# A bias table's load and the first part of its product moved to the head of a hybrid decoder layer

## The chip, the cores and the metric

The kernel runs on one core of a Trainium2 chip. Its metric is the device time of one execution in microseconds (us); of several runs the median counts. The engines are TensorE (PE; its weight loads are shown apart as PEld), VectorE (DVE), ScalarE (ACT), GpSimd (POOL) and SyncE (SP). SP and ACT also issue DMAs, each on a queue of its own: the trace calls SP's q1 and ACT's q10, and marks an issue with SPq or ACTq.

## The reference

One decoder layer on 1024 tokens of width 1024, with 16 meta tokens put in front. Cut to its outline:

```
h = layer_norm(concat([meta, x]), in_ln_g, in_ln_b)
z = h @ w_in + b_in                       # q | k | v | conv value, conv gate | merge gates
# attention: banded blocks of 128 queries, window 128, 16 meta keys, a sink per head
s = q @ k * scale + rel_bias[t5_bucket(q_pos - k_pos)]     # masked outside the window
o = softmax(s, sink) @ v ;  y_attn = o @ w_attn_proj
c = silu(layer_norm(dwconv31(c_val * sigmoid(c_gate)))) @ w_conv_proj
h = layer_norm(ALPHA*h + (sigmoid(g_a)*y_attn + sigmoid(g_c)*c) @ w_out)
f = (gelu(dwconv3(h @ w_up_gate)) * dwconv3(h @ w_up_u)) @ w_down
h = layer_norm(ALPHA*h + f)               # the 16 meta tokens are dropped
```

The bias `rel_bias[t5_bucket(d)]` depends on the distance alone. So the kernel makes one row of 564 values for each of the 8 heads, `vrow`, as a product of two parts of one small table `tab`: 33 rows that hold a one-hot matrix of 564 columns (bucket by distance; row 33 is the mask) and, in 8 more columns, the bias of each bucket and head.

## The kernel before

Everything is float32, and accurate products are made from two halves of each operand (hi and lo, three products for one). Tokens lie in 9 tiles: `xm` holds the meta tokens, and x0 to x7 hold 128 tokens each. The program has a head (to about 54 us), in which the tokens are normalised, turned by PE (transposes at L500) and multiplied by the first three tiles of `w_in` (L547 and L550), then a stretch with the other tiles of `w_in`, the convolution over 31 taps on DVE and the attention (to about 390 us), then the two projections, `w_out` and the feed-forward part.

A scheduler of the framework sets each engine's order of work at build time, by priorities (`rank`, `tc.cur_priority`) and a simulated timeline. In the head the order is written out by hand instead: the wrappers `pe`, `ac`, `dv` and `po` tie each instruction of an engine to the one written before it. PE begins with 23 products of a 128x128 matrix of ones with itself into the tile `ps_w` (L574). Nothing reads them; they occupy PE while the first tokens are loaded and normalised. PE's next instructions are the transposes of `turns(0, ...)`: for each of four column blocks one of `xm` and two of the normalised tiles `xn`. ACT's first instructions in the head are `table(0)`, the inverse root of the meta tokens' variance (L417), which waits for DVE's statistics, and `norm(0, ...)` (L466), which waits for POOL's small steps (`newton(0)`).

The first loads are all SP's, in the order of their ranks: meta tokens, x0, x1, `cols` (biases and the identity matrix of the transposes), a weight tile, x2, x3, x4, two weight tiles, x5, x6, x7, then the table at rank 25 as the 14th, then two `gb` (L113; 512 KB each but for the meta tokens with 64 KB, `cols` with 259 KB and the table with 73.7 KB). Each DMA takes one of eight semaphores in turn (DMAHW0 to DMAHW7 in the rows below), and the DMA that takes the same one again waits for the earlier to land. So SP's 14th DMA, the table, waits for the sixth, x2; the first `gb` for x3, the second `gb` for x4.

The two products of the table stand behind the last product of the head:

```
for a, b in ((0, 400), (400, J_LEN)):                       # J_LEN = 564
    ps = pat.tile([P, 512], F, name="ps_v", tag="o" if a == 0 else "t", bufs=1 if a == 0 else 2)
    after(nc.tensor.matmul(ps[:NH, :b - a], tab[:, J_LEN:], tab[:, a:b], start=True, stop=True), pe_done[-1])
    after(nc.vector.tensor_copy(vrow[:, a:b], ps[:NH, :b - a]), first_nm)
load(v1d, vrow)
```

`vrow` goes to DRAM (`v1d`), from there to 128 copies (`vd`), and from these the skewed bias tiles are loaded, which the attention adds to its scores. All of `tab` but the 33 loaded rows is set to zero by POOL (L204), so the product runs over 128 partitions.

Of the kernel before, what the change touches and what calls it, by code (L numbers as in the profile page):

```python
# [23 lines left out]
F = mybir.dt.float32  # L24
# [5 lines left out]
P = 128  # L30
# [8 lines left out]
NH = 8  # L39
# [29 lines left out]
J_BAND, J_META, J_META0, J_METAQ, J_LEN = 0, 384, 400, 544, 564  # L69
# [32 lines left out]
def tile_hybrid_layer(  # L102
# [3 lines left out]
    nc = tc.nc  # L106
# [5 lines left out]
    def load(o, i):  # L112
        return nc.sync.dma_start(out=o, in_=i)  # L113

    def store(o, i):

        return nc.scalar.dma_start(out=o, in_=i)
# [4 lines left out]
    def after(ins, first):  # L122

        tc.add_manual_dep(ins.ins, first.ins.name, mybir.DependencyInfo(
            mybir.DependencyClass.NoSync, mybir.DependencyReason.SCHED_ONLY), reason="order of work")

    @contextmanager
    def rank(p):

        saved = tc.cur_priority  # L130
        tc.cur_priority = p
        yield
        tc.cur_priority = saved
# [30 lines left out]
    pat = ps_stack.enter_context(tc.tile_pool(name="pat", bufs=1, space=PSUM, reuse_waits="tile"))  # L164
# [3 lines left out]
    start = ExitStack()  # L168
# [33 lines left out]
    tab = sp.tile([P, J_LEN + NH], F, name="tab")  # L202
    with rank(0):
        nc.gpsimd.memset(tab, 0.0)  # L204
    with rank(25):
        load(tab[:33], table_in)

    def bcol(m):
        return colA[:, m:m + 1]
# [189 lines left out]
    def src_of(j):  # L399
        return (xt[j], P) if j >= 0 else (xm[:2 * NMETA], 2 * NMETA)  # L400
# [13 lines left out]
    def table(t):  # L414
        mv, t_, r_, m_ = norms[t]
        n = src_of(tokens[t][0])[1]
        ac(nc.scalar.activation(r_[:n], mv[:n, :, 1], AF.Abs_reciprocal_sqrt, bias=eps[:n], scale=1.0))  # L417

    def half_var(t):
        n = src_of(tokens[t][0])[1]  # L420
        mv, t_ = norms[t][:2]
        put, ts = (po, nc.gpsimd.tensor_scalar) if t < 2 else (dv, V.tensor_scalar)
        put(ts(t_[:n], mv[:n, :, 1], EPS, -0.5, OP.add, OP.mult))

    def newton(t):
        n = src_of(tokens[t][0])[1]
        mv, t_, r_, m_ = (x_[:n] for x_ in norms[t])
        if t < 3:
            put, ts = (po, nc.gpsimd.tensor_scalar) if t < 2 else (dv, V.tensor_scalar)
            put(ts(t_, t_, r_, r_, OP.mult, OP.mult))  # L430
            put(ts(t_, t_, 1.5, r_, OP.add, OP.mult))
            if t < 2:
                put(ts(m_, mv[:, :, 0], -1.0, t_, OP.mult, OP.mult))
            return
        stt = V.scalar_tensor_tensor
        dv(stt(t_, mv[:, :, 1], EPS, r_, OP.add, OP.mult))
        dv(stt(t_, t_, -0.5, r_, OP.mult, OP.mult))
        dv(stt(r_, t_, 1.5, r_, OP.add, OP.mult))
        dv(stt(m_, mv[:, :, 0], -1.0, r_, OP.mult, OP.mult))
# [7 lines left out]
    def norm(t, j, on_dve, cols=range(0, D, 512)):  # L447
        x_, n = src_of(j)
        i = tokens[t].index(j)
        mv, t_, r_, m_ = norms[t]  # L450
        if j < 0:
            xns[j], to = xm, xm[96:]
        elif cols[0]:
            to = xns[j]
        else:
            xns[j] = to = sp.tile([P, D], F, name="xn", tag="xn", bufs=4) if j < 4 else OB[:, (j - 4) * D:(j - 3) * D]
        if t < 3:
            r_ = t_
        for a in cols:
            if on_dve:  # L460
                s1, s2, o1, o2 = r_[:n, i:i + 1], m_[:n, i:i + 1], OP.mult, OP.add
                if t == 2:
                    s1, s2, o1, o2 = mv[:n, i, 0:1], s1, OP.subtract, OP.mult
                dv(V.tensor_scalar(to[:, a:a + 512], x_[:, a:a + 512], s1, s2, o1, o2))
            else:
                ac(nc.scalar.activation(to[:, a:a + 512], x_[:, a:a + 512], AF.Identity, bias=m_[:n, i:i + 1],  # L466
                                        scale=r_[:n, i:i + 1]))
# [102 lines left out]

    tc.cur_priority = RK_START
    warm = pat.tile([P, 512], F, name="ps_w", tag="o")
    for i in range(23):
        pe(nc.tensor.matmul(warm[:, :P], ones, ones, start=True, stop=True))  # L574
    stat(0, -1)
    half_var(0)
    table(0)
    newton(0)
    norm(0, -1, False, (0,))
    stat(1, 0)  # L580
# [64 lines left out]

    tc.cur_priority = RK_RESID + 1000
    vrow = sp.tile([NH, J_LEN], F, name="vrow")
    for a, b in ((0, 400), (400, J_LEN)):
        ps = pat.tile([P, 512], F, name="ps_v", tag="o" if a == 0 else "t", bufs=1 if a == 0 else 2)
        after(nc.tensor.matmul(ps[:NH, :b - a], tab[:, J_LEN:], tab[:, a:b], start=True, stop=True), pe_done[-1])  # L650
        after(nc.vector.tensor_copy(vrow[:, a:b], ps[:NH, :b - a]), first_nm)
    load(v1d, vrow)

# [79 lines left out]
    for r in range(2):  # L733
        rows = slice(r * HD, (r + 1) * HD)

        def put(o, j, skew=1):
            load(o[rows], dram(vd, r * J_LEN + j, [[L8 - skew, HD], [2 * J_LEN, NH // 2], [1, o.shape[-1]]]))
# [8 lines left out]
    ps = pat.tile([P, 512], F, name="ps_vm", tag="t", bufs=2)  # L746
# [4 lines left out]
    for q4 in range(2):  # L751
        ps = pat.tile([P, 512], F, name="ps_v4", tag="t", bufs=2)
# [41 lines left out]
    ps = pat.tile([P, 512], F, name="ps_s2", tag="t", bufs=2)  # L794
    for h in range(NH):
        g, r = divmod(h, 4)
        o = ps[:2, h * 16:(h + 1) * 16]
# [34 lines left out]
    for g in range(NKV):  # L832
        ps = pat.tile([P, 512], F, name="ps_t2", tag="t", bufs=2)
# [6 lines left out]
    for g in range(NKV):  # L840
        o = po[:, g * 8:g * 8 + 8]
# [21 lines left out]
    for i in range(NB):  # L863
        for g in range(NKV):
# [7 lines left out]
            for u in range(2):  # L872
                k0 = 144 * (i - 1) + 16 + HD * u if i else 0
                w = KW - first[u]
                ps = pat.tile([P, 512], F, name="ps_s", tag="s", bufs=2)
                for h in range(2):
                    o = ps[:, h * KW:h * KW + w]
                    for j in range(2):
                        nc.tensor.matmul(o, q[:, j, u, h], kflat[:, k0:k0 + w],
                                         start=j == 0, stop=j == 1)  # L880
# [27 lines left out]
            for n, cols_of in ((P, (0, 80)), (80, (P, 0))):  # L908
                ps = pat.tile([P, 512], F, name="ps_t", tag="t", bufs=2)
# [659 lines left out]
    for c in range(FC):  # L1569
# [8 lines left out]
        for subs in passes:  # L1578
            last = subs == passes[-1]
            w_next = iter(range(7))  # L1580
            a, b = SUB[subs[0]][0], SUB[subs[-1]][1]
            i = max(a, 2)
# [348 lines left out]
```

## Time and profile before

| | |
|---|---|
| median of 3 runs | 1236.25 us (1236.25 to 1236.26) |
| the profiled execution's own time | 1236.54 us |
| its span, first to last instruction | 1234.6 us |
| PE busy | 1225.2 us, 99% of the span |
| DVE busy | 1085.2 us, 88% |
| ACT busy | 584.7 us, 47% |
| mean HBM traffic | 172 GB/s |

The page gives shares of the span for each engine, the span in 40 slices, the DMA queues, the chain of work that ended last and the costliest groups of instructions. Other views are asked of the trace: the waits by engine, the timeline of a short window (start, length, engine, line, tile, and in brackets the idle time before and what ended it), the busy time by windows, and the packets of each DMA queue in a window. Two records of a float32 product stand for one instruction (the 23 idle products are 46 records).

### The profile page before, as it was taken

Reading aid. Unit: us, or ns where it says so; the run is one execution under the profiler, and the core shown is the slowest. Engines: PE = TensorE matmul, PEld = TensorE weight load, DVE = VectorE, ACT = ScalarE, POOL = GpSimd, SP = SyncE. Lnnn points to the kernel's source line nnn. Section 1 sums busy time; section 2 is a strip of 40 time slices with the busy share of each in tenths; the row PEclk is TensorE's granted clock in tenths of the full one; section 3 lists DMA queues with packets and bytes.
Section 4 is the critical chain, followed back from the end, with each engine's and each line's share of the span. In section 5 each row is a group of like instructions: output and inputs, shape, how many; then the busy total and the mean of one; then the engine's idle time right before and its main releaser. Section 6 shows DMA issues by size and latency. Waiting matters only on the chain.

```text
span 1234.6 us, 21810 instructions
## 1 busy us (share of the span) xinstructions
PE 1225.2 (99%) x8568; PEld 1141.5 (92%) x8568; DVE 1085.2 (88%) x1842; ACT 584.7 (47%) x1065; POOL 15.6 (1%) x20
## 2 busy tenths in 40 slices
PE   9999999999999999999999999999999999999997
PEld 8999989999999999888999999999999998888886
DVE  8899989999879798659899999998999986996697
ACT  7532336654255223345755545555455554445331
POOL 1000000000000010000000000000000000000000
PEclk9999999999999999999999999999999999999999
DMA  7396834412255655322255555554455568988722
GB/s 282 74 298 151 210 98 116 127 55 73 82 158 163 183 140 144 104 85 87 66 171 207 191 187 205 188 183 142 172 203 190 178 239 304 391 315 312 256 86 85
DMA packets 109152, 213.02 MB, mean 173 GB/s; under 512 B 31883, under 2 KB 46779, under 8 KB 108922
## 3 DMA queue, kind: packets, MB, share of 16 engines
q1 hardware_dynamic: 93050, 200.56, 49.5%
q10 hardware_dynamic: 16000, 11.07, 2.9%
q8 instruction: 67, 1.10, 0.4%
q14 instruction: 35, 0.29, 0.1%
HBM read 149.98 MB, written 62.70 MB: 172 GB/s over the span
## 4 chain that ended last, share of the span: by engine, by line
PE 98%; DVE 1%; ACT 0%; issue 0%; DMA 0%; POOL 0%; DVEq 0%; POOLq 0%
PE px L1599 14%; PE py L1599 9%; PE ps_x L1745 9%; PE ps_z L315 8%; PE ps_z L314 8%; PE ps_z L310 8%; PE ps_z L1745 8%; PE pw L1599 5%; PE pz L1599 5%; PE ps_p L310 2%; PE ps_p L314 2%; PE ps_p L315 2%; PE ps_w L310 2%; PE ps_w L315 2%; PE ps_w L314 2%; PE ps_z L550 2%
## 5 line engine op out<-in xcount | busy, mean ns | idle before, releaser
L707 DVE SCALAR_TENSOR_TENSOR FA<-cin,cols,FA 128x1026 f32<-128x1026 f32 x120 | 152.2, 1277 | 0.9
L315 PE MATMUL ps_z<-RHO,wlo 128*128 128x256 f32 (+2 forms) x324 | 103.5, 320 | 0.0
L314 PE MATMUL ps_z<-RHO,whi 128*128 128x256 f32 (+2 forms) x324 | 103.4, 319 | 0.0
L315 PE MATMUL ps_z<-RHC,wlo 128*128 128x256 f32 (+2 forms) x324 | 103.4, 319 | 0.0
L314 PE MATMUL ps_z<-RHC,whi 128*128 128x256 f32 (+2 forms) x324 | 103.4, 319 | 0.0
L310 PE MATMUL ps_z<-RHO,whi 128*128 128x256 f32 (+2 forms) x324 | 103.3, 319 | 0.0
L310 PE MATMUL ps_z<-RHC,whi 128*128 128x256 f32 (+2 forms) x324 | 103.2, 319 | 0.0
L279 ACT CAST whi<-wr 128x1024 fp32r<-128x1024 f32 x37 | 38.9, 1050 | 107.4 <-PE ps_z L314 85.5
L1408 ACT CAST RHO<-wr 128x512 fp32r<-128x512 f32 x92 | 55.3, 619 | 25.3 <-DVE wr L1426 11.7
L1409 DVE TENSOR_TENSOR RHO<-wr,RHO 128x512 fp32r<-128x512 f32 x92 | 61.8, 684 | 5.1 <-ACT RHO L1408 5.0
L310 PEld LDWEIGHTS ps_z<-RHO,whi 128*128 128x128 f32 x324 | 60.9, 188 | 4.3
L314 PEld LDWEIGHTS ps_z<-RHO,whi 128*128 128x128 f32 x324 | 61.0, 188 | 4.2
L310 PEld LDWEIGHTS ps_z<-RHC,whi 128*128 128x128 f32 x324 | 60.9, 188 | 4.1
L314 PEld LDWEIGHTS ps_z<-RHC,whi 128*128 128x128 f32 x324 | 61.0, 188 | 4.0
L315 PEld LDWEIGHTS ps_z<-RHO,wlo 128*128 128x128 f32 x324 | 60.9, 188 | 4.0
L315 PEld LDWEIGHTS ps_z<-RHC,wlo 128*128 128x128 f32 x324 | 61.0, 188 | 3.9
L1426 DVE TENSOR_TENSOR wr<-wr 128x512 f32<-128x512 f32 x88 | 59.9, 681 | 0.2
L282 DVE TENSOR_TENSOR wlo<-wr,whi 128x1024 fp32r<-128x1024 f32 x35 | 42.7, 1220 | 11.8 <-ACT whi L279 11.4
L1611 ACT COPY FA<-px 128x514 f32<-128x514 f32 (+2 forms) x23 | 13.2, 572 | 70.7 <-PE px L1599 70.6
L1408 ACT CAST ws<-wr 128x512 fp32r<-128x512 f32 x60 | 36.1, 618 | 18.8 <-DVE wr L1426 10.7
L714 ACT ACTIVATE FA<-ps_z,cols 128x258 f32<-128x258 f32 (+2 forms) x48 | 26.1, 544 | 39.4 <-PE ps_z L315 36.6
L1599 PE MATMUL px<-OA,RHO 128*128 128x258 f32 (+1 forms) x336 | 43.8, 279 | 0.0
(491 smaller groups left out, 3488.2 us busy)
## 6 DMA issues: line engine op xcount, KB each, us to landing
wr<-in_w_up_dram SPq DMA_DIRECT2D x44, 512.0 KB, 4.6
wr<-in_w_z_dram SPq DMA_DIRECT2D x30, 512.0 KB, 3.9
fd<-FA SPq DMA_DIRECT2D x44, 256.0 KB, 2.4
OB<-in_w_down_dram SPq DMA_DIRECT2D x19, 512.0 KB
qt<-qd SPq DMA_DIRECT2D x28, 256.0 KB, 4.1
td<-OB SPq DMA_DIRECT2D x12, 512.0 KB
sums<-fd SPq DMA_DIRECT2D x12, 512.0 KB, 7.6
sd<-sums SPq DMA_DIRECT2D x12, 512.0 KB
```

What stands on the lines that cost most here:

```text
L279: ins = nc.scalar.copy(hi, raw)
L282: return (nc.vector if quick else nc.gpsimd).tensor_tensor(lo, raw, f32(hi), OP.subtract)
L310: ins = nc.tensor.matmul(ps, ah, bh, start=i == 0, stop=False)
L314: nc.tensor.matmul(ps, ah, bl, start=False, stop=False)
L315: last = nc.tensor.matmul(ps, al, bh, start=False, stop=i == n - 1)
L707: nc.vector.scalar_tensor_tensor(acc[c], cin[:, j:j + U], wc, acc[c], OP.mult, OP.add)
L714: nc.scalar.activation(t, ps, AF.Tanh, bias=bcol(14 + i), scale=0.5)
L1408: nc.scalar.copy(hi, src)
L1409: ins = nc.vector.tensor_tensor(lo, src, f32(hi), OP.subtract)
L1426: ins = nc.vector.tensor_tensor(*x)
L1599: ins = nc.tensor.matmul(o, x[:, ks], bmat(sub, q, hl, k), start=first and k + j == 0, stop=k == 3 and j == 2, skip_group_check=not first)
L1745: nc.tensor.matmul(bank[:, cs], l[:, ts], r[:, ws], start=first and a and x + k == 0, stop=z and x == len(ops) - 1 and k == 2, skip_group_ ...
```

## The change

The table's load leaves SP's list and becomes a DMA of ACT, written behind `table(0)`. The idle products become 20. Behind them PE makes the first 512 columns of the table's product, into the bank that `ps_w` had. The other 52 columns stay where both products were. DVE copies the 512 columns as soon as its own head is done, and the 52 columns as before.

```
-    with rank(25):
-        load(tab[:33], table_in)
...
-    for i in range(23):
+    for i in range(20):
         pe(nc.tensor.matmul(warm[:, :P], ones, ones, start=True, stop=True))
     stat(0, -1)
     half_var(0)
     table(0)
+    ac(store(tab[:33], table_in))
+    ps_v0 = pat.tile([P, 512], F, name="ps_v", tag="o")
+    pe(nc.tensor.matmul(ps_v0[:NH], tab[:, J_LEN:], tab[:, :512], start=True, stop=True))
     newton(0)
...
-    for a, b in ((0, 400), (400, J_LEN)):
-        ps = pat.tile([P, 512], F, name="ps_v", tag="o" if a == 0 else "t", bufs=1 if a == 0 else 2)
-        after(nc.tensor.matmul(ps[:NH, :b - a], tab[:, J_LEN:], tab[:, a:b], start=True, stop=True), pe_done[-1])
+    for a, b in ((0, 512), (512, J_LEN)):
+        ps = ps_v0
+        if a:
+            ps = pat.tile([P, 512], F, name="ps_v", tag="t", bufs=2)
+            after(nc.tensor.matmul(ps[:NH, :b - a], tab[:, J_LEN:], tab[:, a:b], start=True, stop=True), pe_done[-1])
         after(nc.vector.tensor_copy(vrow[:, a:b], ps[:NH, :b - a]), first_nm)
```

(`store` issues a DMA from ACT, `load` from SP.) In the changed kernel line numbers between L207 and L574 are two lower, and from L651 on three higher.

PE at the start of the program, before (with what each instruction waits for; the DMAHW names are the DMAs' semaphores):

```order
L574 MATMUL ps_w<-ones_r 128x128 [waits DVE_49]
L574 MATMUL ps_w<-ones_r 128x128 x22
L500 MATMUL ps_h_216<-cols,xm 128x128 [waits DMAHW0_49,DMAHW3_49,DVE_49,Activation_49]
L500 MATMUL ps_h_216<-cols,xn 128x128 [waits Activation_49]
L500 MATMUL ps_h_216<-cols,xn 128x128 [waits DVE_49]
```

PE at the same place, now:

```order
L572 MATMUL ps_w<-ones_r 128x128 [waits DVE_49]
L572 MATMUL ps_w<-ones_r 128x128 x19
L578 MATMUL ps_v<-tab 8x512 [waits DMAHW7_49,PE_49,Pool_49]
L498 MATMUL ps_h_215<-cols,xm 128x128 [waits DMAHW0_49,DMAHW3_49,DVE_49,Activation_49]
L498 MATMUL ps_h_215<-cols,xn 128x128 [waits Activation_49]
```

The table's product stands ahead of all transposes and waits for the table's DMA (DMAHW7).

ACT at the start of the program, before (`sq` is a first call that loads ACT's function table, `r_...` an inverse root, `xm` the meta tokens):

```order
L174 ACTIVATE sq<-eps 128x1 [waits DVE_49]
L417 ACTIVATE r_172<-mv_170,eps 32x1 [waits DVE_49]
L466 ACTIVATE xm<-xm,m_173,t_171 32x512 [waits DMAHW0_49,Pool_49]
L417 ACTIVATE r_186<-mv_184,eps 128x1 [waits DVE_49]
L466 ACTIVATE xm<-xm,m_173,t_171 32x512
```

ACT at the same place, now:

```order
L174 ACTIVATE sq<-eps 128x1 [waits DVE_49]
L415 ACTIVATE r_168<-mv_166,eps 32x1 [waits DVE_49]
L117 DMA tab<-in_table_dram 33x572 [waits Pool_49]
L464 ACTIVATE xm<-xm,m_169,t_167 32x512 [waits DMAHW0_49,Pool_49]
L415 ACTIVATE r_185<-mv_183,eps 128x1 [waits DVE_49]
```

The DMA stands behind the first inverse root, which waits for DVE, and itself waits only for POOL's clearing of the tile.

SP's list of loads in the head, before, from the eighth DMA on (`x_113` is x4, `wr` are weight tiles):

```order
L113 DMA x_113<-in_x_dram 128x1024
L113 DMA wr_142<-in_w_z_dram 128x1024 [waits DMAHW0_49]
L113 DMA wr<-in_w_z_dram 128x1024 [waits DMAHW1_49]
L113 DMA x_115<-in_x_dram 128x1024 [waits DMAHW2_49]
L113 DMA x_117<-in_x_dram 128x1024 [waits DMAHW3_49]
L113 DMA x_119<-in_x_dram 128x1024 [waits DMAHW4_49]
L113 DMA tab<-in_table_dram 33x572 [waits DMAHW5_49,Pool_49]
L113 DMA gb<-in_ln_dram 128x1024 [waits DMAHW6_49,DVE_49]
L113 DMA gb<-in_ln_dram 128x1024 [waits DMAHW7_49,Activation_49]
```

SP's list, now:

```order
L113 DMA x_113<-in_x_dram 128x1024 [waits DMAHW0_49]
L113 DMA wr_141<-in_w_z_dram 128x1024 [waits DMAHW1_49]
L113 DMA wr<-in_w_z_dram 128x1024 [waits DMAHW2_49]
L113 DMA x_115<-in_x_dram 128x1024 [waits DMAHW3_49]
L113 DMA x_117<-in_x_dram 128x1024 [waits DMAHW4_49]
L113 DMA x_119<-in_x_dram 128x1024 [waits DMAHW5_49]
L113 DMA gb<-in_ln_dram 128x1024 [waits DMAHW6_49,DVE_49]
L113 DMA gb<-in_ln_dram 128x1024 [waits DMAHW7_49,Activation_49]
```

The table is gone from the list, and since its DMA on ACT takes the eighth semaphore, each load from x4 to x7 waits for a load one place later than before.

Behind the head the scheduler's order moves too, on every engine, through the attention. For example PE at the first four transposes of v (`ps_v_...`, L755), before, among the products of the other tiles of `w_in` (`ps_z`):

```order
L314 MATMUL ps_z<-RHC,whi 128x512
L315 MATMUL ps_z<-RHC,wlo 128x512
L755 MATMUL ps_v_789<-cols,FA 128x128 x4
L310 MATMUL ps_z<-RHO,whi 128x272
L314 MATMUL ps_z<-RHO,whi 128x272
```

PE at the same place, now:

```order
L313 MATMUL ps_z<-RHC,wlo 128x512
L758 MATMUL ps_v_786<-cols,FA 128x128 x4
L308 MATMUL ps_z<-RHC,whi 128x512
L312 MATMUL ps_z<-RHC,whi 128x512
L313 MATMUL ps_z<-RHC,wlo 128x512
L308 MATMUL ps_z<-RHO,whi 128x272
```

The same instructions stand there, the transposes three products earlier.

## The prediction

> **What bounds the kernel now.** I read the page first, then PE's waits, then PE's share of single windows.
>
> ```profile
> span 1234.6 us, 21810 instructions
> PE 1225.2 (99%) x8568; PEld 1141.5 (92%) x8568; DVE 1085.2 (88%) x1842; ACT 584.7 (47%) x1065; POOL 15.6 (1%) x20
> PE 98%; DVE 1%; ACT 0%; issue 0%; DMA 0%; POOL 0%; DVEq 0%; POOLq 0%
> ```
>
> ```profile
> PE ps_w L574 <- DVE ones_r L222: 1.1, 1, 1.1
> PE ps_h L500 <- ACT xn L466: 0.6, 1, 0.6
> PE pw L1599 <- DVE OA L1284: 0.4, 1, 0.4
> ```
>
> ```profile
> 90.00:120.00 30.00, 30.00 (x202) 27.65 (x202) 29.37 (x32) 9.11 (x16) 0.00 (x0) 1.00 0.68 152
> 700.00:800.00 100.00, 100.00 (x872) 100.00 (x871) 95.08 (x157) 52.27 (x88) 0.00 (x0) 1.00 0.55 190
> ```
>
> PE bounds it: 98% of the chain that ended last. Its waits in the whole program are three, 2.1 us together (columns: total, times, longest), and the first two lie in the head, at PE's start and at the first transpose that needs a normalised tile. From there PE is busy all of every window. Two things follow. Work taken from PE behind the head shortens the run by its length. And a wait put into PE's head lengthens the run by its length, for no idle time comes later to take it up.
>
> The head decides, so I read its timeline (start, length; SPq and ACTq rows are DMA issues).
>
> ```profile
> 1.08 7.71 PE L574 MATMUL ps_w<-ones_r 128*128 128x128 f32 x46 [1.08 <-DVE ones_r L222]
> 3.07 1.85 SPq L113 DMA_DIRECT2D x<-in_x_dram  x3
> 4.65 0.29 ACT L417 ACTIVATE r<-mv,eps 32x1 f32<-32x1 f32 x1 [2.41 <-DVE mv L412]
> 4.96 1.46 SPq L113 DMA_DIRECT2D wr<-in_w_z_dram  x2
> 6.19 0.81 ACT L466 ACTIVATE xm<-xm,m,t 32x512 f32<-32x512 f32 x1 [1.25 <-POOL m L433]
> 8.63 0.27 PE L500 MATMUL ps_h<-cols,xm 128*128 128x128 f32 x1
> 9.47 0.33 PE L500 MATMUL ps_h<-cols,xn 128*128 128x128 f32 x1 [0.57 <-ACT xn L466]
> ```
>
> The idle products fill PE to 8.63 us, and real work is dense from 9.47 us. The new product must be through by about 9.3 us to cost nothing, so the question is when the table lands.
>
> **When the table lands.** ACT takes its instructions in order, so it reaches the DMA when the inverse root at 4.65 us has got its input. Two rows show what a DMA of ACT does behind big loads of SP. ACT issued a store of `kd` at 17.15 us and one of `sgd` at 163.37 us:
>
> ```profile
> 17.15 0.35 ACTq L117 DMA_DIRECT2D kd<-FA  x1
> q1 hardware_dynamic: 382, 1.32, 101.9%
> ...
> q1 hardware_dynamic: 158, 0.55, 73.4%
> q10 hardware_dynamic: 144, 0.14, 21.3%
> 162.10 0.35 SPq L113 DMA_DIRECT2D wr<-in_w_z_dram  x1
> 163.37 0.33 ACTq L117 DMA_DIRECT2D sgd<-FA  x1
> q1 hardware_dynamic: 80, 0.33, 73.1%
> ...
> q1 hardware_dynamic: 49, 0.15, 45.6%
> q10 hardware_dynamic: 100, 0.09, 34.1%
> 34.87 0.34 ACTq L117 DMA_DIRECT2D kd<-FA  x1
> DMA packets 0, 0.00 MB, mean 0 GB/s; under 512 B 0, under 2 KB 0, under 8 KB 0
> q10 hardware_dynamic: 135, 0.18, 54.0%
> ```
>
> The queue rows (packets, MB, share) belong to windows. From 17.15 to 20.55 us only SP's q1 moves, 1.32 MB of loads issued before; ACT's q10 has its 144 packets between 20.6 and 22.5 us. From 163.4 to 164.88 us again only q1 moves, the weight load issued at 162.10 us, and q10 begins in the window 164.9 to 165.7 us. With nothing ahead, the store issued at 34.87 us moves nothing up to 35.65 us and most of its bytes from 35.7 us on: 0.8 us. So a DMA of ACT waits 3.4 us and 1.5 us where loads of SP are under way, until these are done, against 0.8 us. I take it that the two queues are served in the order of issue.
>
> At 4.65 us SP has issued eight loads, the last x4 (the three issues from 3.07 us are x2, x3 and x4, ending at 4.92 us); the weight tiles come at 4.96 us. So the table stands behind x4. When x4 lands is seen from SP, whose next issues wait for x2, x3 and x4 in turn:
>
> ```profile
> 10.51 0.36 SPq L113 DMA_DIRECT2D tab<-in_table_dram  x1
> 11.72 1.54 SPq L113 DMA_DIRECT2D gb<-in_ln_dram  x2
> 12.94 0.33 SPq L113 DMA_DIRECT2D gb<-in_ln_dram  x1
> ```
>
> x2 has landed by 10.51 us, x3 by 11.72 us, x4 by 12.94 us: 1.2 us for each 512 KB. The table's 73.7 KB add 0.17 us, and SP's own waking, which is in these times, takes about as much off. I take 12.9 us.
>
> The Trainium skill says otherwise: "DMA: Bandwidth & Descriptors", section "Queues, rings and completion order", has each DMA engine take turns, packet by packet, between the queues that have work, which would bring the table in within some 2 us. The two stores above do not agree with that, for ACT's queue got no turn in 3.4 us; the first rival keeps the rule all the same.
>
> **The change part by part.**
>
> *The product in the head.* PE's 20 products end three earlier: six records of (8.5 − 5.7) / 24 = 0.117 us (rows below), so at 8.63 − 0.7 = 7.9 us. Then PE waits for the table to 12.9 us. The product's price comes from the float32 products of 272 columns, and the one of 400 and 164 columns is seen where it stands now:
>
> ```profile
> 13.98 4.17 PE L547 MATMUL ps_z<-FA,wr 128*128 128x272 f32 x18
> 54.10 1.12 PE L650 MATMUL ps_v<-tab 128*8 128x400 f32 x4
> 55.15 0.28 PE L747 MATMUL ps_vm<-cols,FA 128*16 128x128 f32 x1
> ```
>
> 18 records in 4.17 us are 0.232 us each; 512 columns cost 2 × 0.232 × 512/272 = 0.87 us. Work that began at 9.47 us before, behind one transpose of 0.11 us, begins at 12.9 + 0.87 + 0.11 = 13.9 us: **+4.4 us**. The three idle products that go save nothing, since PE would only wait longer.
>
> *The clock.* The idle products at the start show what a cold PE costs, and the program's end what makes it cold:
>
> ```profile
> L574 PE MATMUL ps_w<-ones_r x20: 391/421/421, 1.7 to 5.7; 128*128 128x128 f32 x20
> L574 PE MATMUL ps_w<-ones_r x25: 275/275/391, 5.7 to 8.5; 128*128 128x128 f32 x25
> 1226.86 0.52 PE L1745 MATMUL ps_z<-RHO 128*128 128x256 f32 x3
> 1231.00:1233.00 2.00, 0.00 (x0) 0.00 (x0) 0.49 (x1) 0.00 (x0) 0.00 (x0) 0.58 0.67 251
> 1233.00:1235.00 2.00, 0.00 (x0) 0.00 (x0) 0.00 (x0) 0.00 (x0) 0.00 (x0) 0.50 0.03 11
> ```
>
> Records start every (5.7 − 1.7) / 19 = 0.21 us at first and every 0.117 us later; the slow stretch runs from 1.08 to 5.7 us. At the end PE stops at 1227.4 us, and a mean granted clock (the column before the last two) of 0.58 over the window from 1231 us puts the fall to 0.50 at 1231.3 us, after 3.9 us of idleness. The wait made here is 12.9 − 7.9 = 5.0 us. So the clock may fall, and the work behind it, product included, loses between nothing and 4.6 × (1 − 0.117/0.21) = 2.0 us. One sight of the fall and a margin of 1.1 us don't settle it; I take the middle, **+1.0 us**. The skill's page "TensorE: Matmul & The Clock Gate", section "Part 1: The HAM clock gate", has the clock fall after a whole idle window of 3.4 us of a free-running count and return after a busy one; by it a fall would lose about 1.6 us (an estimate), and whether it comes depends on where the count stands.
>
> *The two products behind the head.* They take PE from 54.10 to 55.15 us, 1.05 us; 52 columns in two records cost at least one weight change each, some 0.1 to 0.3 us. I take 0.2: **−0.85 us**.
>
> *The rest, at nothing.* ACT's issue (0.35 us) lies in its idle time between 4.94 and 6.19 us; without it the first `xm` step would slip by 0.35 us, and PE has 0.57 us there. SP's loads x5 to x7 wait one load longer, about 1.2 us, covered by the queue ahead of them; uncovered it would be that 1.2 us on x5, which is needed only in the second half of the head. The copy of 512 columns on DVE runs beside PE. The scheduler's new order behind the head moves products among products; PE waited for nothing there, so it can't gain, and I take 0, with a bound in the last rival.
>
> Sum: 4.4 + 1.0 − 0.85 = **+4.55 us**. Against the profiled execution's own 1236.54 us that is 1241.1; the median of the runs shown is 0.3 us lower, so I forecast **1240.8 us**, with 1239.8 if the clock holds and 1241.8 if it falls.
>
> **The rivals.**
>
> 1. *The table lands in time (not slower).* If ACT's DMA gets turns at once, or if ACT runs ahead of the waiting inverse root and issues before SP has issued so much, the table is there by 7.9 us. Point of decision: landing before about 8.5 us (9.47 − 0.11 − 0.87). The product ends by 8.8 to 9.3 us, the first transpose still meets its `xn` at 9.47 us, and only −0.85 us is left: 1235.4 us. For it speaks the skill's rule above, against it both stores.
> 2. *The table overtakes x4*, since SP is still issuing it at 4.65 us. Then it lands at 11.7 us; PE idles 3.8 us, less than 3.9, and the clock holds: 4.4 − 1.2 − 0.85 = +2.35 us, 1238.6 us.
> 3. *The next weight tile gets ahead of it* (SP's issues around 4 to 6 us take 0.6 us and more, as if they queued). Landing 14.1 us, with the clock's fall: 4.4 + 1.2 + 2.0 − 0.85 = +6.75 us, 1243.0 us.
> 4. *The new order makes PE wait in the attention.* PE's longest wait behind the head is 0.4 us; six such would be 2.4 us on top of the forecast: 1243.2 us. Nothing in the profile speaks for it but that DVE is 29.37 of 30 us busy from 90 us on.
>
> **How the numbers follow.** Forecast 0.50, rivals 0.12, 0.10, 0.15 and 0.13. A difference of 0.2% (2.5 us) is about what a measurement can tell from none. Forecast, third and fourth rival are slower by more: 0.78. The second and nearly all of the first are within: 0.20. Left for faster: 0.02, since only 0.85 us of PE's work can go. The range reaches from just below the second rival to just above the fourth, 1238.3 to 1243.6 us; it leaves out the first rival.
>
> **What would show it.** In the changed profile: an idle time of about 5 us before `ps_v` on PE, ended by the table's DMA; no packet of q10 before about 11.5 us; the first transpose at about 13.8 us; the first records behind the wait with 0.21 us pitch if the clock fell; 52 columns in 0.2 us behind the head; no other new wait on PE. The prediction is wrong if `ps_v` starts before 9 us, or if the span grows while PE's wait before `ps_v` is short.

## The result and the profile after

The changed kernel takes 1242.86 us (median of 6 runs, 1241.62 to 1244.63) against 1236.25 us (1236.07 to 1236.33) of the kernel before: 1.0056 times as long, 95% interval 1.0043 to 1.0069. The forecast was 1240.8 us, 1238.3 to 1243.6. Sign and range were right. The make-up of the sum was not: the head cost less than half of what was forecast, and a place that was put down at nothing cost more than the head.

The profiled execution took 1242.87 us, 6.33 us more than the profiled one of before. The page first, then PE's waits:

```profile
span 1240.9 us, 21795 instructions
PE 1227.1 (99%) x8562; PEld 1142.9 (92%) x8562; DVE 1085.5 (87%) x1842; ACT 584.0 (47%) x1065; POOL 15.6 (1%) x20
PE 94%; DMA 2%; DVE 2%; ACT 1%; issue 1%; DVEq 0%; SPq 0%; ACTq 0%
```

```profile
PE ps_z L308 <- DVE cin L701: 2.6, 1, 2.6
PE ps_v L578 <- DMA tab<-in_table_dram: 2.0, 1, 2.0
PE ps_w L572 <- DVE ones_r L220: 1.1, 1, 1.1
PE px L1602 <- ACT OB L1614: 0.5, 1, 0.5
PE pw L1602 <- DVE OA L1287: 0.4, 1, 0.4
```

PE does a little more busy time than before (1227.1 against 1225.2 us) with six records fewer, and its chain falls from 98% to 94%: part of the loss is waiting, part is slower work. Three waits are new. The table's, in the head, is 2.0 us; the longest is another, 2.6 us for `cin` on DVE; a third of 0.5 us stands at 598 us.

**The head.** The timeline of its issues and of PE (start, length):

```profile
3.07 1.42 SPq L113 DMA_DIRECT2D x<-in_x_dram  x3
4.63 0.61 ACTq L117 DMA_DIRECT2D tab<-in_table_dram  x1
10.43 1.02 PE L578 MATMUL ps_v<-tab 128*8 128x512 f32 x2 [2.00 <-DMA tab<-in_table_dram]
11.55 0.38 PE L498 MATMUL ps_h<-cols,xn 128*128 128x128 f32 x2
55.99 0.26 PE L653 MATMUL ps_v<-tab 128*8 128x52 f32 x2
56.18 0.28 PE L750 MATMUL ps_vm<-cols,FA 128*16 128x128 f32 x1
```

The first transpose of `xn` comes at 11.55 us in place of 9.47: +2.08 us. At the head's end the 52 columns take 56.18 − 55.99 = 0.19 us where the two products took 1.05, and the next instruction (`ps_vm`) stands at 56.18 in place of 55.15 us: net **+1.03 us**. The DMA queues' rows (packets, MB, share) for 0 to 8.5 us and then for 8.5 to 9.7 us show the table arriving:

```profile
q1 hardware_dynamic: 705, 2.30, 76.7%
...
q1 hardware_dynamic: 116, 0.41, 85.4%
q10 hardware_dynamic: 44, 0.08, 16.5%
```

The loads that SP issued before 4.63 us are the meta tokens, x0 to x4, `cols` and one weight tile, 3.5 MB by their sizes. When the table's packets start, 3.9 us behind their issue, 2.30 MB have moved; when the last of them ends, at 9.65 us, 2.71 MB. So by these sums the table passed x4 and about half of x3, 0.8 MB that was issued earlier, and still waited behind what was nearest. PE starts the product at 10.43 us, 0.8 us behind the last packet.

**Near 80 us.** Here VectorE's order decides. Before, on DVE (`cin` is the convolution's input, made from PE's result bank; `wlo` is the low half of a weight tile):

```profile
76.49 0.87 DVE L698 SCALAR_TENSOR_TENSOR cin<-ps_z,cols,FA 128x272 f32<-128x272 f32 x2
78.42 0.75 DVE L698 SCALAR_TENSOR_TENSOR cin<-ps_z,cols,FA 128x512 f32<-128x512 f32 x1 [1.06 <-PE ps_z L315]
80.56 1.22 DVE L282 TENSOR_TENSOR wlo<-wr,whi 128x1024 fp32r<-128x1024 f32 x1
```

After, on ACT, DVE and PE:

```profile
79.19 1.04 ACT L277 CAST whi<-wr 128x1024 fp32r<-128x1024 f32 x1 [8.85 <-PE ps_z L312]
80.26 1.23 DVE L280 TENSOR_TENSOR wlo<-wr,whi 128x1024 fp32r<-128x1024 f32 x1 [2.31 <-ACT whi L277]
81.41 1.55 DVE L701 SCALAR_TENSOR_TENSOR cin<-ps_z,cols,FA 128x272 f32<-128x272 f32 x3
81.95 0.60 PE L308 MATMUL ps_z<-RHO,whi 128*128 128x272 f32 x1 [2.57 <-DVE cin L701]
```

The scheduler now puts the seventh weight tile's `wlo` ahead of the `cin` copies. `wlo` waits for ACT's `whi`; that cast waits until PE is through with the tile's buffer, at 79.2 us; and PE's next product waits for a result bank, which only the first `cin` copy, queued behind `wlo`, gives back. PE stands still for **2.57 us**. The windows behind it (columns: PE, PEld, DVE, ACT and POOL busy, then the granted clock, DMA share and GB/s):

```profile
78.27:81.68 3.41, 1.11 (x5) 0.56 (x3) 1.42 (x2) 1.47 (x3) 0.00 (x0) 1.00 0.86 334
81.68:85.09 3.41, 3.13 (x14) 3.14 (x15) 3.41 (x12) 0.10 (x1) 0.00 (x0) 0.50 1.03 420
85.09:88.50 3.41, 3.41 (x30) 3.41 (x30) 3.35 (x10) 1.66 (x4) 0.00 (x0) 1.00 1.02 411
```

PE works 3.13 us at half clock, half of which is lost: **+1.6 us**. The sum: 1.03 + 2.57 + 1.57 + 0.47 (the wait at 598 us) = 5.6 of 6.33 us; the remaining 0.7 us lies in amounts that no wait row shows.

### The profile page after: what moved, and what is told of

The parts are those of the page before. It is cut to its first block, busy times and chain, and to the rows that moved or that the text cites. A ratio compares the mean times of both kernels' runs of the same rounds, so it can differ in the third digit from the quotient of the medians.

```text
span 1240.9 us, 21795 instructions
## 1 busy us (share of the span) xinstructions
PE 1227.1 (99%) x8562; PEld 1142.9 (92%) x8562; DVE 1085.5 (87%) x1842; ACT 584.0 (47%) x1065; POOL 15.6 (1%) x20
## 4 chain that ended last, share of the span: by engine, by line
PE 94%; DMA 2%; DVE 2%; ACT 1%; issue 1%; DVEq 0%; SPq 0%; ACTq 0%
PE px L1602 14%; PE py L1602 9%; PE ps_x L1748 9%; PE ps_z L308 8%; PE ps_z L312 8%; PE ps_z L313 8%; PE ps_z L1748 8%; PE pw L1602 5%; PE pz L1602 5%; PE ps_p L308 2%; PE ps_p L312 2%; PE ps_p L313 2%; PE ps_w L313 2%; PE ps_w L308 2%; PE ps_w L312 2%; PE ps_z L548 2%
```

## The experiments

Theory H, before the first four: the added time is PE's wait for the table, plus VectorE's exchanged order near 80 us with the half clock behind it, and nothing else. The rivals stand with each run. Ratios are to the kernel before, run on the same chip.

**The load alone.** The kernel before, with only the table's load moved to ACT; both products where they were.

```
-    with rank(25):
-        load(tab[:33], table_in)
...
     table(0)
+    ac(store(tab[:33], table_in))
     newton(0)
```

> Only the load moves to ACT's queue; 23 idle products and both products of the table behind the head stay. Theory H (the added time is PE's wait for the table in the head plus a new order of DVE's copies around 80 us): nothing waits for the table early, so 1236.2 us, within 0.3 us of before. Rival (the load itself or SP's later semaphores slow the head): 1237.5 us or more, with a new wait of PE in the first 30 us.

Measured: 1236.33 us (1236.21 to 1236.56, 11 runs), ratio 1.0001 (0.9992 to 1.0009). The move of the load costs nothing: SP's shifted loads and ACT's issue were rightly put at zero. VectorE's order near 80 us stays the old one, so it is the rest of the change (the product's move, with three idle products fewer), not the load's move, that brings the exchange. Why the scheduler makes it was not traced.

**The changed kernel with VectorE's old order near 80 us.** One dependency puts the seventh tile's `wlo` behind the third `cin` copy.

```
+        if n == 7:
+            after(last_split[-1], cin_done[2])
...
-            nc.vector.scalar_tensor_tensor(cin[:, 16 + a:16 + b], ...)
+            cin_done.append(nc.vector.scalar_tensor_tensor(cin[:, 16 + a:16 + b], ...))
```

> The changed kernel with one order fixed: DVE's split of the seventh weight tile comes behind the three copies from PSUM into cin, as it did before the change. Theory H: the 2.6 us wait of PE near 80 us and the half clock behind it are gone, the wait of 2 us for the table stays, so 1236.25 + 2.08 (head) - 1.05 (shorter products) = 1237.3 us, 1238.0 at most. Rival (the wait moves to another place of the new order): 1240 us or more, with a wait of over 1 us on PE elsewhere.

Measured: 1240.2 us (1237.93 to 1243.42, 9 runs), ratio 1.0032 (1.0023 to 1.0042). The profiled execution was the shortest, 1237.93 us, and is as H has it: the wait for `cin` is gone, the clock never falls, and PE waits for the table alone.

```profile
PE ps_v L581 <- DMA tab<-in_table_dram: 1.9, 1, 1.9
```

But the median is 2.3 us above that, and the executions spread over 5.5 us at mean clocks from 0.999 down to 0.995, while the kernel before stays within 1.3 us in 25 runs. H explained one execution, not the kernel; something that H leaves out varies.

**The exchange alone.** The kernel before, with the three `cin` copies put behind the seventh tile's `wlo`; table and products untouched.

```
+        if n == 7:
+            for ins in cin_done[:3]:
+                after(ins, last_split[-1])
```

> The kernel before, with DVE's three copies into cin put behind the split of the seventh weight tile, as the changed kernel has them; nothing else is changed. Theory H: PE waits some 2.6 us near 78 us, and where the clock falls to half for a window of 3.4 us another 1.4 us go: 1238.9 to 1240.5 us. Rival (that order is free and the loss comes from the head alone): 1236.3 us.

Measured: 1240.72 us (1239.39 to 1241.25, 5 runs), ratio 1.0034 (1.0021 to 1.0046). PE's waits and the windows behind the long one:

```profile
PE ps_z L314 <- DVE cin L702: 2.6, 1, 2.6
PE ps_s L883 <- DMA qt<-qd: 0.6, 1, 0.6
```

```profile
78.43:81.84 3.41, 1.21 (x9) 1.21 (x10) 2.87 (x5) 0.90 (x3) 0.00 (x0) 1.00 1.03 420
81.84:85.26 3.42, 3.42 (x17) 3.42 (x16) 3.30 (x6) 0.37 (x1) 0.00 (x0) 0.50 1.03 417
```

The same wait, the same window at half clock, with table and head as in the kernel before: 4.4 us in the median. The dependency moves other work too (DVE's `kx` casts now stand ahead of `wlo`, and PE's order differs from about 172 us on), but the loss is in place before that: the product that PE starts at 85.15 us in the kernel before starts at 89.46 us here, 4.3 us later. That settles the second cost. A wait of 0.6 us for `qt` comes with it: the attention's first product needs a tile that goes through DRAM and has little time to spare.

**The table loaded earlier.** The changed kernel with the old order near 80 us, and ACT's DMA written ahead of `table(0)`, so that ACT issues it at 2.34 us.

```
+    ac(store(tab[:33], table_in))
     table(0)
-    ac(store(tab[:33], table_in))
```

> As the changed kernel with the fixed order, but ACT's DMA of the table stands ahead of its first inverse root, so it is issued at about 2.3 us, behind x0, x1 and cols only. Theory H: the table lands by 7 us, the product follows the 20 idle products without a wait, the first needed transpose starts at 9.5 us as before, and only the shorter products behind the head are left: 1236.25 - 0.85 = 1235.4 us. Rival (the product in the head costs by itself, or ACT's queue is served late whatever is ahead): 1236.5 us or more.

Measured: 1236.33 us (1235.18 to 1236.7, 11 runs), ratio 0.9999 (0.9990 to 1.0008). With the table in time and the old order, both costs are gone. The gain of 0.85 us isn't there in the median. The profiled execution has it, with `ps_vm` at 54.06 us and a span of 1233.6 us, and so have two others (1233.4 and 1233.7 us); most have spans of 1234.1 to 1234.4 us, as before.

**The early load with the exchanged order.** The same without the dependency.

> The changed kernel with ScalarE's load of the table issued at 2.3 us, ahead of table(0), and VectorE's order near 80 us as the change leaves it. Theory H (the swap's price stands by itself): the product starts near 7.7 and the first transpose of xn near 9.3 as in the kernel with the early load and the old order (1236.33 us), then PE waits 2.6 us for cin near 80 us and runs a window of 3.4 us at half clock, 1.4 to 1.5 us more: 1236.3 + 4.0 to 4.5 = 1240.3 to 1240.8. Rival: the wait near 80 us comes from the later head and goes with it: 1236.3 to 1237.

Measured: 1240.51 us (1239.04 to 1242.12, 6 runs), ratio 1.0033 (1.0022 to 1.0045), as H had it; the wait does not come from the late head. (The head itself is not quite as forecast: in the profile the idle products end at 8.74 us, because the clock rises only at 7.24 us, and the product starts at 8.84 us, not near 7.7.) The profiled execution, at 1239.04 us the shortest, has the wait of 2.6 us and no window at half clock:

```profile
PE ps_z L308 <- DVE cin L701: 2.6, 1, 2.6
```

```profile
75.51:78.92 3.41, 2.31 (x11) 1.55 (x9) 1.06 (x2) 1.30 (x3) 0.00 (x0) 1.00 0.91 270
78.92:82.34 3.42, 1.95 (x15) 1.95 (x16) 3.42 (x7) 0.17 (x1) 0.00 (x0) 1.00 0.99 405
```

These windows are cut where the clock's steps fall, all whole multiples of 3.41 us apart in a trace. Here the same wait lies across a boundary: 1.1 us of idleness in one window, 1.5 in the next, and the clock holds. In the exchange alone and in the changed kernel 2.2 and 2.3 us of it lay in one window, and the clock fell. So one wait costs 2.6 or about 4.2 us, by where the windows stand in that execution.

**What varies in the head.** Theory C puts the pinned kernel's spread down to the clock, theory L to the table's landing. Two kernels change the idle time ahead of the table's product, with the old order near 80 us: 26 idle products in place of 20, and 12.

```
-    for i in range(20):
+    for i in range(26):
```

> The changed kernel with VectorE's old order near 80 us, and 26 idle products in place of 20 ahead of the table's product; no other instruction moves but one pair of transposes. In the kernel with 20, PE stood 1.9 us idle for the table and the executions spread from 1237.9 to 1243.4 us, at clocks from 0.999 to 0.995. Theory C (that idle time makes the clock fall, or rise later, in those executions whose windows of 3.4 us it fills far enough): six more products of 0.21 us leave 0.6 us idle, the table's product starts as before near 10.5, the clock stays at 0.998 to 0.999 in every execution and the time is 1237.3 to 1238.3 in all of them. Rival L (the table lands later in some executions, and the clock follows from the wait): the spread stays, median near 1240, highest above 1242. Rival S (the spread has nothing to do with the head): the same as L in time, with the profile's head as C has it.

Measured: 1239.37 us (1238.35 to 1240.3, 10 runs), ratio 1.0024 (1.0015 to 1.0033). The spread shrinks from 5.5 to 2.0 us, and the long executions are gone, as C has it. But C's 1237.3 to 1238.3 us isn't met, and the median's 0.8 us below that of 20 products is within the two intervals. PE's waits of the profiled execution (1239.36 us) show what C left out:

```profile
PE ps_s L885 <- DMA qt<-qd: 1.1, 1, 1.1
PE ps_v L581 <- DMA tab<-in_table_dram: 0.8, 1, 0.8
```

With 12 idle products:

> The same with 12 idle products: PE is done with them near 6.2 us and idle 4.3 us until the table's product near 10.5. Theory C: in the head no window of 3.4 us is busy all through before the table's product, so the granted clock goes up at 13 to 17 us in place of 7, and each 3.4 us at half clock behind 10.5 costs 1.7 us: 1239.3 to 1241.5 us, with less spread than the kernel with 20. Rivals L and S: the product starts when the table lands, near 10.5, as before, and idle time ahead of it costs nothing more: median near 1240 with the spread from 1238 to 1243 unchanged.

Measured: 1241.53 us (1239.89 to 1241.95, 5 runs), ratio 1.0039 (1.0026 to 1.0053). The idle time of 4.1 us makes the clock fall for two windows:

```profile
6.26:9.68 3.42, 0.23 (x2) 0.02 (x1) 2.66 (x8) 3.22 (x6) 1.03 (x4) 1.00 0.98 385
9.68:13.09 3.41, 2.55 (x6) 0.88 (x7) 2.98 (x7) 0.27 (x1) 0.00 (x0) 0.50 1.02 419
13.09:16.50 3.41, 3.41 (x16) 3.07 (x15) 1.63 (x7) 2.31 (x4) 0.00 (x0) 0.50 1.03 422
```

Half of 2.55 + 3.41 us is 3.0 us lost; `ps_vm` stands 2.8 us later than in the shortest execution with 20 products. So C's mechanism is shown, for hardly more than the count of idle products differs. Its details were not: the clock did not rise late, at 13 to 17 us, but rose at 6.26 us, fell at 9.68 us and came back at 16.50 us. The window of 9.68 us, three quarters busy, did not bring the clock back; the one behind it, wholly busy, did.

**The kernel with 20 products and the old order, twice more,** for profiles of longer executions.

> The pinned changed kernel once more, for a profile of an execution above 1239. Theory C: where the time is above 1239, the granted clock falls to 0.5 in the head behind the wait for the table, or stays low there longer, by one window of 3.4 us (1.7 us) or two; up to 1.1 us more is a wait of the first ps_s for qt near 140 us, as in the kernel with 26 idle products; 1237.9 with neither. Rival L: ScalarE's first packet starts later than 8.5 us by as much as the time is above 1237.9, the clock steady.

> As the one before it: the sum of 1237.9, of 1.7 for each window of 3.4 us that the clock spends at 0.5 in or behind the head beyond its rise near 7 us, and of the wait for qt, within 0.4 us. Rival L as there.

Measured: 1239.46 and 1239.84 us. The first has a steady clock and two waits:

```profile
PE ps_v L581 <- DMA tab<-in_table_dram: 3.1, 1, 3.1
PE ps_s L885 <- DMA qt<-qd: 0.5, 1, 0.5
```

Here the table lands later. The product's start in the shortest execution, then here:

```profile
10.57 1.02 PE L581 MATMUL ps_v<-tab 128*8 128x512 f32 x2 [1.91 <-DMA tab<-in_table_dram]
11.36 1.02 PE L581 MATMUL ps_v<-tab 128*8 128x512 f32 x2 [3.11 <-DMA tab<-in_table_dram]
```

With that, 1237.93 + 0.8 + 0.5 is 1239.2 us. That is L's mechanism, though not by L's sign: q10's first packet comes at 8.50 us, as in the shortest execution (8.45 us), and it is the last that ends later, at 10.33 in place of 9.54 us. The second has C's:

```profile
7.96:11.38 3.42, 0.68 (x2) 0.12 (x2) 2.47 (x6) 1.81 (x3) 0.31 (x2) 1.00 1.02 407
11.38:14.79 3.41, 3.41 (x14) 2.92 (x14) 3.31 (x11) 1.79 (x4) 0.00 (x0) 0.50 1.03 422
```

PE is busy only 0.68 us of one window and loses half of the next, 1.7 us: 1237.93 + 1.7 + 0.1 (a start at 10.70 us) is 1239.7 us. Its wait of 3.3 us is long mainly because the idle products ended early, at 7.4 us, the clock having risen at 4.55 us. So both theories hold in part: the table's landing varies, and the wait for it, 1.9 to 3.3 us in these three profiles, can cost the clock on top. Rival S holds in part too, for the wait for `qt`, 0.5 to 1.1 us in three of the pinned kernels' profiles (with 12, 20 and 26 products), lies near 140 us. No execution above 1240 us of the kernel with 20 products was profiled, so what made the longest (1243.42 us) stays open.

**What a DMA of ACT waits for.** The kernel with the early load and the old order, and a second load of the table into a tile that nobody reads, behind `table(1)`.

```
     table(1)
+    probe = sp.tile([33, J_LEN + NH], F, name="probe")
+    ac(store(probe, table_in))
```

> The changed kernel with the early load and VectorE's old order, and a second load of the same table into a tile that nobody reads, issued by ScalarE near 7 us, when SP has 12 loads of 128 rows issued and more than 1 MB is still on its way. So far the first packet of ScalarE's queue started 3.4 us (issue at 2.34) and 3.9 us (issue at 4.63) behind the issue. Theory Q (what each DMA engine has already taken, some 20 packets, goes first, the rest of SP's queue does not): first packet 3.4 to 4.2 us behind the issue, near 11. Rival O (order of issue over all queues, as the prediction had it): behind the last packet of the loads of x issued before it, near 15 to 16. Rival R (the queues take turns packet by packet, nothing else ahead): within 1 us of the issue, near 8. The time by all three: that of the kernel without it, 1235.8 to 1236.4.

The issue, and the queue rows for 6.9 to 10.5 us and 10.5 to 12 us (the two packets of q10 in the first are the end of the first load):

```profile
7.13 0.31 ACTq L117 DMA_DIRECT2D probe<-in_table_dram  x1
```

```profile
q1 hardware_dynamic: 410, 1.49, 102.2%
q10 hardware_dynamic: 2, 0.00, 0.0%
...
q1 hardware_dynamic: 148, 0.54, 88.6%
q10 hardware_dynamic: 44, 0.08, 13.2%
```

The first packet starts at 10.56 us, 3.4 us behind the issue, as theory Q has it. Order of issue (near 15 us) and turns from the start (near 8 us) are both out. Over all traces with the load on ACT, issued from 2.34 to 7.13 us, the delay is 2.9 to 4.0 us, and q1 moves 1.0 to 1.4 MB in that time. The store of `sgd` in the kernel before, 1.5 us behind 0.33 MB, speaks for an amount ahead and against a fixed delay. That the DMA engines had already taken just these packets is Q's explanation; no trace shows it.

This kernel's single run, 1236.73 us, also shows how a lead is lost. It had `ps_vm` 0.73 us earlier than before (54.42 us), and then two waits that the kernel before does not have among its three:

```profile
592.10 1.70 PE L1607 MATMUL px<-OC,RHO 128*128 128x256 f32 x12 [0.43 <-ACT OB L1619]
599.08 1.18 PE L1607 MATMUL py<-RHC,ws 128*128 128x256 f32 x8 [0.24 <-ACT OB L1619]
```

0.67 us of the 0.73 is given back there. That the other executions with the early load lose theirs at the same place is likely but not shown.

No version tried beats the kernel before.

## Why the prediction was right in its sum and wrong in its parts

*What bounds the kernel:* right for waits: those put into PE's time came out as run time, in the head and at 80 us. "Work taken from PE behind the head shortens the run by its length" did not come out as simply. With the early load only three of eleven executions kept the gain, and in the last profile above two waits near 592 and 599 us took 0.67 us of a lead of 0.73 us.

*When the table lands* was the first step that failed: "I take it that the two queues are served in the order of issue." PE could start the product at 10.43 us, not 12.9, and the head cost 2.08, not 4.4 us. PE idled 2.0 us, not 5.0; 0.5 us of that difference is the idle products, which ended at 8.43 us and not at 7.9, because the clock rose at 6.59 us in this execution and at 5.95 us in the one before. The two stores were read rightly, but they couldn't tell order of issue from a limited amount ahead: ahead of `kd` 1.32 MB moved in 3.4 us, which is both nearly all that was queued (1.44 MB by the loads' sizes) and just the amount that goes first here. The second rival, overtaking x4, came nearest, but gave 11.7 us. The Trainium skill, "DMA: Bandwidth & Descriptors", section "Queues, rings and completion order", has each DMA engine take turns between queues. The trace agrees that later work of another queue passes earlier work of SP's, about 0.8 MB of it, and disagrees with the landing within 2 us that the prediction drew from the rule: 2.9 to 4.0 us pass before the first packet.

*The clock:* the step that read the fall as one "after 3.9 us of idleness" failed. In the head of the profiled execution PE idled 2.0 us and the clock held (term +1.0, measured 0); behind the 2.57 us near 80 us it fell, which cost 1.6 us. In the pinned kernel it fell in the head too, in one of three profiles. What counts is idleness inside one window, not its length as such. The page "TensorE: Matmul & The Clock Gate", section "Part 1: The HAM clock gate", of the Trainium skill has a free-running window of 3.4 us; the trace agrees, steps lie 3.41 us or a multiple apart and stand differently in each execution. It has the clock fall after an idle window; here windows with 0.68, 1.11 and 1.21 us of PE's work in them were enough, and the measurement decides.

*The two products behind the head:* −0.85 forecast, 1.05 − 0.19 = 0.86 us measured. Right.

*The rest at nothing:* right for ACT's issue and SP's loads (the load alone costs nothing). Wrong for the new order, and this is the largest of the failed steps: "PE waited for nothing there, so it can't gain, and I take 0". A place without waits can lose by any reordering. The fourth rival named this kind with six waits of 0.4 us in the attention; it came as one wait of 2.57 us ahead of the attention, with 1.6 us of half clock behind it. The profile did hold a warning: the row of before at 78.42 us shows DVE ready 1.06 us early for the last `cin` copy, so there PE and DVE hand banks to each other with about 1 us of slack, and the order of DVE around that row was what to compare.

By the terms: head 4.4 forecast and 2.08 measured, clock in the head 1.0 and 0, products −0.85 and −0.86, new order 0 and 4.14 (2.57 + 1.57), and 0.97 us unassigned. Of that 0.47 us is the wait at 598 us; no run shows that it comes from the new order, and the kernel with the second load, where DVE has its old order near 80 us, has a like wait at the same line. (The sum above leaves 0.7 us, because it counts this wait and has `ps_vm` 1.03 us later, not 2.08 − 0.86 = 1.22.) Two terms were together 3.3 us too high, and 5.1 us were not forecast at all; so the sum was only 1.8 us off. That the range held is luck: errors of opposite sign cancelled.

The prediction's own signs say the same. Only the 52 columns in 0.2 us came as written. The idle time was 2.0 us and not about 5, q10's first packet came at 8.5 us and not behind 11.5, the first transpose at 11.55 us and not 13.8, and PE had two other new waits, one of them longer than the table's.

## What to carry to other kernels

When an edit lets a scheduler reorder work, compare the order of every engine that gives buffers back to the bound one, not only the bound engine's own: one instruction put ahead of a copy that frees a bank cost more here than the edit itself. A load on a second queue isn't late by all that the first queue holds, but it isn't free of it either; the delay is measured by its first packet, and issuing it 2.3 us earlier removed nearly the whole wait (in the three profiles PE stood idle for at most 0.3 us before the product). A wait on TensorE of 2 us and more should be priced twice, with and without a window at half clock, since the same wait costs either from one execution to the next.

## What the runs showed of the hardware

TensorE's clock changed only at times that lie whole multiples of 3.41 us apart within a trace, and these times stand differently in each execution. Windows with up to 1.83 us of idle time (kernel with 20 products and the old order, 7.07 to 10.48 us) left it at full; windows with 2.20, 2.30, 2.74 and 3.19 us were each followed by one at half. In these runs the point lies between 1.83 and 2.20 us; where, they don't tell. A window at half cost about half of PE's busy time in it (1.6 us for 3.13 us near 82 us).

ScalarE's DMA queue, beside a busy queue of SP, had its first packet 2.9 to 4.0 us behind the issue (3.4, 3.9 and 3.4 us for issues at 2.34, 4.63 and 7.13 us), and passed what SP had queued beyond that (about 0.8 MB in the changed kernel). With nothing ahead the store at 34.87 us moved its first bytes after some 0.8 us.
